# Five places of a streamed hybrid encoder layer: a flush of put-off work, copies of T, steps around the solve, the sums of one post, loads of the embedding blocks

## The chip, the cores and the metric

The kernel runs on one core of a Trainium2 chip. The metric is the device time of one execution in microseconds (us); smaller is better. A core has a matrix engine (TensorE, PE in the profile; its weight loads are PEld), VectorE (DVE), ScalarE (ACT), GpSimd (POOL) and SyncE (SP, which here only issues transfers).

## The reference, cut to what matters

512 rows of `x` and 16 meta rows ahead of them make 528 positions of 1024 features. One layer is computed: a layer norm of the embedding, two mixers side by side (stick-breaking attention over 8 heads of 64, and an RWKV-7 recurrence over 8 heads of 64), their gated sum through `w_out`, a layer norm with the residual, a mixture of 16 experts of which each position takes 2, and a last layer norm.

```python
h = layer_norm(concat([meta, x]), emb_ln_g, emb_ln_b)
p = h @ w_in                       # q, k, v, p_rw, gate_sb, gate_rw
o_sb = stick_breaking_attention(q, k, v)
x = p_rw + (token_shift(p_rw) - p_rw) * mu       # r, k, v, wd, ad, gd
w = exp(-DECAY_SCALE * sigmoid(w0 + tanh(wd) @ w_up)); a = sigmoid(a0 + ad @ a_up); g = sigmoid(gd) @ g_up
# for each t:  S = S*w_t + (S @ -kk_t)(kk_t*a_t)^T + v_t k_t^T ;  y_t = S @ r_t
o_rw = (group_norm(y)*lnx_g + lnx_b + (r*k*r_k).sum()*v) * g
merged = sigmoid(gate_sb) * (o_sb @ p_sb) + sigmoid(gate_rw) * (o_rw @ p_rwkv)
h = layer_norm(ALPHA*h + merged @ w_out, ln1_g, ln1_b)
h = layer_norm(ALPHA*h + MoE(h), ln2_g, ln2_b);  return h[16:]
```

## The kernel before

**Products in three parts.** A product in float32 is made of three matmuls on rounded numbers: both sides are split into a high part (`_hi`, a copy that rounds, on ScalarE, line L109) and a low part (`_lo`, what is left, a subtraction on VectorE or GpSimd, line L237), and high by high, high by low and low by high are added up in one bank of TensorE's result memory.

**The stream.** Every large projection from the embedding (and later the merge's) is a job of 8 steps in one list, `ST`. A step (L329) is three matmuls with a 128x128 block of weights. A job has two halves of four steps. At the first step of half h the load of half h+3 is issued on SP (`w_raw`, L267); at the second step half h+2 is split (`w_hi` on ScalarE, `w_lo` on GpSimd, or partly on VectorE where `ST.dve` says so). `ST.later(n, f)` puts a piece of work off until n more steps are issued. So the order in which the program issues work is written out by hand, and each engine runs its own instructions in that order; nothing is rearranged on the chip.

**drive.** Stages that leave TensorE idle (RWKV's preparation, the solve, the chain, the posts) are generators. `drive` runs such a stage and, at each `yield d`, issues steps until the debt d is paid; a step pays 0.66. A yield of 1.0 thus brings two steps or one, by what is owed already, one of 4.0 six or so. The 16 gate jobs (`gate`, 128 steps) are what is left for the solve and the chain. At the end of a gate job ScalarE makes a sigmoid, GpSimd multiplies it with the attention's part and a transfer writes it to memory.

**The order of the stages.** Attention (18 rounds with six streamed steps each); up to the end of job `xv0`; LoRA's weights and inputs are converted (L703, L704, and L766, L767 in `lora`); RWKV's preparation in four pairs; `solve`; `chain`; the posts; the merge; `w_out`; router; experts. `shift_mix` makes RWKV's shifted inputs: ScalarE scales two banks, and the addition on VectorE (L520) is put off by `MIX` = 2 steps, and frees the banks.

**solve.** It inverts triangular blocks. VectorE makes `T` row by row (L955 to L957). Three copies of it on ScalarE follow (`T0`, twice `Tf`), then VectorE's merges into `Xc` and `Tf`, four transposes (L984, `T32`; L988, the last of `U`), two memsets on GpSimd (L990), which wait for L988 since they write to `U` too, and a yield of `SY[0]`. Then come two rounds of 32 small matmuls each: L1000 (on `LM` and `T32`), a copy on ScalarE, a yield of `SY[1]`, L1010 (on `Xs` and `U`), a copy, a yield of `SY[2]`.

**chain and posts.** `chain` runs the recurrence over nine chunks for two groups of head pairs; it begins with a yield of `CHY[2]`. `post(b)` normalizes 128 positions of the output `ORW`: L1104 to L1112 (mean, square, variance), L1118 (scale and offset), L1119 (add the bonus; on GpSimd for b < 3), L1121 (multiply by the gate; VectorE). Three posts begin within the chain. `posts` ends them, and starts the fourth, and splits `ORW` into `orw_hi` and `orw_lo` (`in_parts`, L1127), parts 0 to 2 on GpSimd, part 3 on VectorE.

**merge.** Jobs `m0` to `m5` work through `MERGES`, pairs of a block m of 128 output columns and a part of the positions (`L1188`; in L1192 to L1195 VectorE multiplies the bank by the gate, adds attention's part, ScalarE makes `hT_hi`, VectorE `hT_lo`). In the loop over m = 0 to 9 ahead of `w_out` (L1311), `wsplit_by` splits the weights of `w_out` in put-off pieces (L1242 on VectorE), `wraw` loads more of them, and at m = 1, 3, 5, 7 (`HBM`) one block of the embedding, `hb[b]`, is loaded back (L1328), and multiplied by `emb_ln_g` and shifted by `emb_ln_b` on VectorE (L1329, L1330), of which the rows are loaded at m = 1. The experts' loads (`fetch`, 1 MB each on SP) begin at m = 7.

Of the kernel before, what the change touches and what calls it, by code (L numbers as in the profile page):

```python
# [13 lines left out]
AF = mybir.ActivationFunctionType  # L14
OP = mybir.AluOpType
# [17 lines left out]
DE = 512  # L33
CAP = 32

CHY = (0.0, 0.66, 4.0, 7)
GS = (2, 3, 4, 7)
PST = 9
YPL = (2, 1)
# [3 lines left out]
MIX = 2  # L43
MD = 4
SOLVE_RATE = 1.0
SY = (1.0, 1.4, 1.4)
WARM = 16
WARM_R = (8, 12)
HSD = 4
OVT = 6  # L50
LY = 6
HBM = (1, 3, 5, 7)
FAT = (7, 7, 8, 9)
WOT = (2, 2), (4, 3), (2, 3)
ROT_W = [0, 1, 3, 6, 7]
# [13 lines left out]
def trunk(ctx, tc, A, out):  # L69
    nc = tc.nc  # L70
# [4 lines left out]
    h_d = dram.tile([SEQ, D], FT, name="h_d")  # L75
# [180 lines left out]
    class Stream:  # L256
# [19 lines left out]
        def step(self):  # L276
            h, u = divmod(self.n, 4)
            if h >= 2 * len(self.jobs):
                return
            if u == 0:  # L280
                self.load(h + 3)
            if u == 1:
                self.split(h + 2)
            self.jobs[h // 2][1](self.w.get(h), self.n % 8)
            self.n += 1
            due = [f for n, f in self.hooks if n <= self.n]
            self.hooks = [k for k in self.hooks if k[0] > self.n]
            for f in due:
                f()

        def run(self, n, upto=None):
# [11 lines left out]
    ST = Stream()  # L303
# [374 lines left out]
    for n in range(18):  # L678
        i = n % 4
# [14 lines left out]
        if 0 <= n - 2 < 16:  # L694
            next(live[n - 2])
    ST.upto("xv0")
    lora_w = AT.tile([128, 2, 512], FT, name="lora_w", bufs=1)
    nc.sync.dma_start(lora_w[0:64, 0], A["w_up"][0])
    nc.sync.dma_start(lora_w[64:128, 0], A["a_up"][0])
# [227 lines left out]
    def solve():  # L927
# [22 lines left out]
        Tf = TB  # L950
        nc.gpsimd.memset(Tf[:, 0:16, 16:32], 0.0)
        pr_ = PX.tile([128, 1024], FT, name="pr", tag="xrk", bufs=2)
        for t in range(2, 16):
# [2 lines left out]
                                    Lc[:, :, t, None, 0:t].to_broadcast([128, 3, t, t]), op=OP.mult)  # L956
            nc.vector.tensor_reduce(T[:, :, t, 0:t], pr, axis=AX.X, op=OP.add)  # L957
            yield 0.4 + t * t * 0.0063
        act(T0[:, :, 16:32], T[:, 2], AF.Copy)
        act(Tf[:, 0:16, 0:16], T[:, 0], AF.Copy)  # L960
        act(Tf[:, 16:32, 16:32], T[:, 1], AF.Copy)
        Xc = RW.tile([128, 16, 16], FT, name="Xc", tag="t_G")

        def merge(dst, x, y, i0, i1, j0, j1, k0, k1):
# [8 lines left out]
        for i in (0, 8):  # L973
            merge(Xc, TA[:, 16:32, 0:16], T[:, 0], i, i + 8, 0, 8, 0, 16)
            yield 2.5
            merge(Xc, TA[:, 16:32, 0:16], T[:, 0], i, i + 8, 8, 16, 8, 16)
            yield 1.45
        for i, n in ((0, 8), (8, 16)):
            for j in range(0, 16, 128 // n):
                merge(Tf[:, 16:32, 0:16], T[:, 1], Xc, i, i + 8, j, j + 128 // n, 0, n)  # L980
                yield 2.5
# [115 lines left out]
    def post(b, room):  # L1097

        ts = slice(128 * b, 128 * b + 128)
        y = ORW[:, :, ts]  # L1100
        four = "p (h t) -> p h t"
        s2, bg = room(b)
        for i in range(2):
            nc.sync.dma_start(bg[i], bg_d[:, i, :, ts].rearrange("h p t -> p h t"))  # L1104
        pm = sm()
        nc.tensor.matmul(pm, bones, y, start=True, stop=True)
        yield YP
        nc.vector.scalar_tensor_tensor(y, pm.rearrange(four, h=4), -1.0 / 64, y, op0=OP.mult, op1=OP.add)
        act(s2, y, AF.Square)
        yield YP  # L1110
        pv = sm()
        nc.tensor.matmul(pv, bones, s2, start=True, stop=True)  # L1112
        act(s2, pv.rearrange(four, h=4), AF.Ln, bias=eps_x, scale=1.0 / 64)
        yield YP
        act(s2, s2, AF.Exp, scale=-0.5)
        nc.vector.tensor_tensor(y, y, s2, op=OP.mult)
        for hp in range(4):
            nc.vector.tensor_scalar(y[:, hp], y[:, hp], col("lnx_g", hp), col("lnx_b", hp), op0=OP.mult, op1=OP.add)  # L1118
        (nc.vector if b == 3 else nc.gpsimd).tensor_tensor(y, y, bg[0], op=OP.add)  # L1119
        yield YP  # L1120
        nc.vector.tensor_tensor(y, y, bg[1], op=OP.mult)  # L1121
        yield YP
# [15 lines left out]
    def posts():  # L1138

        for u in PR[0]["posts"]:  # L1140
            for _ in u:
                pass
        late = post(3, late_room)
        in_parts(0, nc.gpsimd)
        yield YPL[0]
        for i in range(5):
            next(late)
            if i in (0, 2):
                WR.append(wraw(wo_units[i // 2], i // 2))
            if i < 2:  # L1150
                in_parts(i + 1, nc.gpsimd)
            yield YPL[1]
        in_parts(3, nc.vector)

# [161 lines left out]
    for m in range(10):  # L1316
        if m < 8:
            ST.run(m_done[m] - ST.n)
            if m == 0:
                WO.append(wsplit_by(WR.pop(0), *WOT[1]))  # L1320
            if m in (2, 4):
                WR.append(wraw(wo_units[1 + m // 2], 1 + m // 2))
            if m == HBM[0]:
                for nm, t in (("emb_ln_g", egr), ("emb_ln_b", ebr)):
                    nc.sync.dma_start(t, bass.AP(tensor=A[nm].tensor, offset=A[nm].offset, ap=[[0, 128], [1, D]]))
            if m in HBM:
                b = HBM.index(m)
                nc.sync.dma_start(hb[b], h_d[b * 128:(b + 1) * 128, :])  # L1328
                nc.vector.tensor_tensor(hb[b], hb[b], egr, op=OP.mult)  # L1329
                nc.vector.tensor_tensor(hb[b], hb[b], ebr, op=OP.add)  # L1330
            if m == 4:
                WO.append(wsplit_by(WR.pop(0), *WOT[2]))
# [458 lines left out]
    with tc.For_i(0, n_1, 1) as _:  # L1791
# [43 lines left out]
        with tc.For_i(0, n_x, 1) as j:  # L1835
# [52 lines left out]
            y = hb[1]  # L1888
# [45 lines left out]
```

## Time and profile before

| what | value |
|---|---|
| executions shown, us | 889.43, 889.32, 882.3 |
| their median, us | 889.32 |
| the profiled execution, us | 883.24 |
| its span in the profile, us | 881.4 |
| its mean granted TensorE clock | 0.956 |
| busy: TensorE, VectorE, ScalarE, GpSimd | 92%, 48%, 36%, 34% |
| TensorE's weight loads (beside its matmuls) | 60% |

The profile is of one execution. Its span runs from its first instruction to its last. The difference to the execution's time lies around it. Busy shares are over the whole span; the stages differ. PEclk is the TensorE clock that the chip granted, as a share of full speed (1.00 is 2.4 GHz, 0.50 is 1.2 GHz).

### The profile page before, as it was taken

Reading aid. Unit: us, or ns where it says so; the run is one execution under the profiler, and the core shown is the slowest. Engines: PE = TensorE matmul, PEld = TensorE weight load, DVE = VectorE, ACT = ScalarE, POOL = GpSimd, SP = SyncE. Lnnn points to the kernel's source line nnn. Section 1 sums busy time; section 2 is a strip of 40 time slices with the busy share of each in tenths; the row PEclk is TensorE's granted clock in tenths of the full one; section 3 lists DMA queues with packets and bytes.
Section 4 is the critical chain, followed back from the end, with each engine's and each line's share of the span. In section 5 each row is a group of like instructions: output and inputs, shape, how many; then the busy total and the mean of one; then the engine's idle time right before and its main releaser. Section 6 shows DMA issues by size and latency. Waiting matters only on the chain. (4 is left out here: it accounts for less than half of the span.)

```text
span 881.4 us, 16057 instructions
## 1 busy us (share of the span) xinstructions
PE 807.7 (92%) x6476; PEld 527.5 (60%) x6476; DVE 421.5 (48%) x791; ACT 317.7 (36%) x639; POOL 299.5 (34%) x343
## 2 busy tenths in 40 slices
PE   7989899879998989979997889999999999999993
PEld 6877777867888867757665777783333333333331
DVE  7565664741467669982464668730112212302304
ACT  6465565554666575435455222111010010010000
POOL 4265765751442444865454000111101300300102
PEclk8998898999999999989999899989999999999996
DMA  4511111135433225434226679689799999999800
GB/s 148 189 51 49 48 49 49 48 100 203 147 98 97 84 74 156 126 115 132 62 62 199 221 247 368 252 314 331 247 387 387 371 386 387 378 385 387 316 1 27
DMA packets 127234, 169.17 MB, mean 192 GB/s; under 512 B 7106, under 2 KB 62476, under 8 KB 127156
## 3 DMA queue, kind: packets, MB, share of 16 engines
q1 hardware_dynamic: 122228, 158.00, 52.1%
q10 hardware_dynamic: 2944, 5.90, 1.8%
q0 software_dynamic: 1984, 4.21, 1.4%
q8 instruction: 52, 0.85, 0.4%
q14 instruction: 26, 0.21, 0.1%
HBM read 152.29 MB, written 17.89 MB: 193 GB/s over the span
## 5 line engine op out<-in xcount | busy, mean ns | idle before, releaser
L237 POOL TENSOR_TENSOR w_lo<-w_raw,w_hi 128x512 fp32r<-128x512 f32 x87 | 119.8, 1378 | 160.4 <-ACT w_hi L109 147.8
L1710 PE MATMUL bank<-raw,x 128*32 128x512 f32 x1536 | 170.8, 594 | 1.9 <-ACT hid L109 1.2
L329 PE MATMUL bank<-hT_hi,w_hi 128*128 128x264 f32 (+1 forms) x512 | 149.4, 348 | 4.1 <-ACT w_hi L109 2.7
L329 PE MATMUL bank<-hT_hi,w_lo 128*128 128x264 f32 (+1 forms) x512 | 139.1, 328 | 4.4 <-POOL w_lo L237 4.4
L329 PE MATMUL bank<-hT_lo,w_hi 128*128 128x264 f32 (+1 forms) x512 | 138.1, 326 | 0.0
L1710 PEld LDWEIGHTS bank<-raw,x 128*32 128x32 f32 x1536 | 47.6, 110 | 105.1 <-issue 102.6
L329 PEld LDWEIGHTS bank<-hT_hi,w_hi 128*128 128x128 f32 x512 | 87.6, 194 | 18.9 <-ACT w_hi L109 4.2
L329 PEld LDWEIGHTS bank<-hT_hi,w_lo 128*128 128x128 f32 x512 | 87.5, 194 | 11.6 <-POOL w_lo L237 6.5
L329 PEld LDWEIGHTS bank<-hT_lo,w_hi 128*128 128x128 f32 x512 | 87.3, 194 | 7.5
L1721 PE MATMUL bank<-raw,h 128*32 128x512 f32 x768 | 87.0, 594 | 0.0
L1684 POOL TENSOR_TENSOR ln_f<-ln_f,mhalf 128x1 f32<-128x1 f32 x12 | 11.5, 955 | 184.6 <-DVE ln_f L1683 184.6
L109 ACT ACTIVATE w_hi<-w_raw 128x512 fp32r<-128x512 f32 x100 | 62.3, 624 | 18.7 <-DMA w_raw<-in_w_in_dram 6.5
L1639 DVE SCALAR_TENSOR_TENSOR hid<-hid,gat,bank 128x512 f32<-128x512 f32 x12 | 9.0, 747 | 121.2 <-PE bank L1710 64.5
L1721 PEld LDWEIGHTS bank<-raw,h 128*32 128x32 f32 x768 | 23.4, 110 | 50.8 <-issue 50.8
L562 POOL TENSOR_TENSOR R<-zs,R 128x144 f32<-128x144 f32 (+3 forms) x32 | 44.9, 1421 | 19.1 <-DVE R L560 19.1
L1311 PE MATMUL bank<-raw,hT_hi 128*128 128x512 f32 x128 | 45.5, 412 | 2.7 <-ACT hT_hi L109 2.7
L109 ACT ACTIVATE h<-bank 128x512 f32<-128x512 f32 x12 | 7.2, 597 | 97.5 <-PE bank L1629 97.5
L109 ACT ACTIVATE x<-bank 128x512 f32<-128x512 f32 x14 | 8.4, 597 | 82.8 <-PE bank L1629 74.3
L1457 POOL TENSOR_TENSOR ln_rs<-ln_ve,mhalf 128x1 f32<-128x1 f32 x4 | 5.3, 1328 | 89.9 <-DVE ln_ve L1456 89.9
L109 ACT ACTIVATE hid<-bank 128x512 f32<-128x512 f32 x12 | 7.1, 595 | 72.2 <-PE bank L1710 72.2
L560 DVE TENSOR_TENSOR_SCAN R<-ones_r,ab 128x144 f32<-128x144 f32 (+3 forms) x32 | 31.8, 1035 | 0.0
L1613 POOL DMA_INDIRECT hb<-h_d,idx x12 | 12.4, 1029 | 54.1 <-DVE idx L1591 36.9
(349 smaller groups left out, 1352.7 us busy)
## 6 DMA issues: line engine op xcount, KB each, us to landing
raw<-in_exp_w_gate_dram SPq DMA_DIRECT2D x32, 1024.0 KB
raw<-in_exp_w_up_dram SPq DMA_DIRECT2D x32, 1024.0 KB
raw<-in_exp_w_down_dram SPq DMA_DIRECT2D x32, 1024.0 KB
w_raw<-in_w_in_dram SPq DMA_DIRECT2D x84, 256.0 KB
raw<-in_w_out_dram SPq DMA_DIRECT2D x4, 1024.0 KB
sig_d<-sg ACTq DMA_DIRECT2D x8, 264.0 KB
sig<-sig_d SPq DMA_DIRECT2D x8, 264.0 KB
xin<-in_x_dram SPq DMA_DIRECT2D x4, 512.0 KB
```

Source lines behind the costliest of these rows:

```text
L109: ins = nc.scalar.activation(out, in_, func, **kw)
L237: eng.tensor_tensor(lo[:, ks], raw[:, ks], hi[:, ks].bitcast(FT), op=OP.subtract)
L329: nc.tensor.matmul(pt[:, :e - s], w_[:, k % 4, :], m[:, k, s:e], start=(k == 0 and n == 0), stop=(k == KD - 1 and n == 2))
L560: nc.vector.tensor_tensor_scan(R[:, h, :W][:, ::-1], ones_r[:, :W], ab[:, h, :W][:, ::-1], 0.0, op0=OP.mult, op1=OP.add)
L562: nc.gpsimd.tensor_tensor(R[:, h, :W], z[:, h], R[:, h, :W], op=OP.subtract)
L1311: nc.tensor.matmul(pt, MG[x][:, k, 128 * b:128 * b + 128], w[y][:, k % 4, :], start=(k == 0 and i == 0), stop=(k == 7 and i == 2))
L1457: nc.gpsimd.tensor_tensor(rs, ve, mhalf, op=OP.pow)
L1613: nc.gpsimd.indirect_dma_start(out=t[:idx.shape[0]], out_offset=None, in_=src, in_offset=bass.IndirectOffsetOnAxis(ap=idx.bitcast(U32), ax ...
L1639: nc.vector.scalar_tensor_tensor(hid, hid, gate, pu, op0=OP.mult, op1=OP.mult)
L1684: nc.gpsimd.tensor_tensor(rs, ve, mhalf, op=OP.pow)
L1710: nc.tensor.matmul(P[k[0]][32 * i:32 * i + 32], x_of(t, i, kk), W[k, e][0][:, s], start=kk == 0, stop=kk == 7)
L1721: nc.tensor.matmul(Y[g, p // 2][r:r + 32], H[t][:, s, 32 * i:32 * i + 32], W[unit_of(k, i), e][0][:, s], start=s == 0 and not second, stop ...
```

## The change

Five edits. First, `ST.flush()`, a new method that runs all work put off so far, is called right behind `ST.upto("xv0")`. Second, the three copies of `T` on ScalarE move behind the merges into `Xc` (four yields later). Third, `SY[0]` goes from 1.0 to 5.0 and `CHY[2]` from 4.0 to 0. Fourth, the sum L1119 of post 2 goes from GpSimd to VectorE, and the low parts 0, 1 and 2 too; the parts 0 and 1 are issued ahead of the call that makes post 3, part 2 at its turn i = 1. Fifth, the loads of the embedding blocks and of the two rows get their own places, m = 0, 1, 3, 5 (`HBL`) and the rows m = 0, while the products stand at m = 2, 3, 5, 7 (`HBM`).

```diff
--- before.py
+++ after.py
@@ -33,7 +33,7 @@
 DE = 512
 CAP = 32
 
-CHY = (0.0, 0.66, 4.0, 7)
+CHY = (0.0, 0.66, 0.0, 7)
 GS = (2, 3, 4, 7)
 PST = 9
 YPL = (2, 1)
@@ -43,13 +43,13 @@
 MIX = 2
 MD = 4
 SOLVE_RATE = 1.0
-SY = (1.0, 1.4, 1.4)
+SY = (5.0, 1.4, 1.4)
 WARM = 16
 WARM_R = (8, 12)
 HSD = 4
 OVT = 6
 LY = 6
-HBM = (1, 3, 5, 7)
+HBL, HBM = (0, 1, 3, 5), (2, 3, 5, 7)
 FAT = (7, 7, 8, 9)
 WOT = (2, 2), (4, 3), (2, 3)
 ROT_W = [0, 1, 3, 6, 7]
@@ -286,6 +286,12 @@
             due = [f for n, f in self.hooks if n <= self.n]
             self.hooks = [k for k in self.hooks if k[0] > self.n]
             for f in due:
+                f()
+
+        def flush(self):
+
+            due, self.hooks = self.hooks, []
+            for _, f in due:
                 f()
 
         def run(self, n, upto=None):
@@ -694,6 +700,7 @@
         if 0 <= n - 2 < 16:
             next(live[n - 2])
     ST.upto("xv0")
+    ST.flush()
     lora_w = AT.tile([128, 2, 512], FT, name="lora_w", bufs=1)
     nc.sync.dma_start(lora_w[0:64, 0], A["w_up"][0])
     nc.sync.dma_start(lora_w[64:128, 0], A["a_up"][0])
@@ -956,9 +963,6 @@
                                     Lc[:, :, t, None, 0:t].to_broadcast([128, 3, t, t]), op=OP.mult)
             nc.vector.tensor_reduce(T[:, :, t, 0:t], pr, axis=AX.X, op=OP.add)
             yield 0.4 + t * t * 0.0063
-        act(T0[:, :, 16:32], T[:, 2], AF.Copy)
-        act(Tf[:, 0:16, 0:16], T[:, 0], AF.Copy)
-        act(Tf[:, 16:32, 16:32], T[:, 1], AF.Copy)
         Xc = RW.tile([128, 16, 16], FT, name="Xc", tag="t_G")
 
         def merge(dst, x, y, i0, i1, j0, j1, k0, k1):
@@ -975,6 +979,9 @@
             yield 2.5
             merge(Xc, TA[:, 16:32, 0:16], T[:, 0], i, i + 8, 8, 16, 8, 16)
             yield 1.45
+        act(T0[:, :, 16:32], T[:, 2], AF.Copy)
+        act(Tf[:, 0:16, 0:16], T[:, 0], AF.Copy)
+        act(Tf[:, 16:32, 16:32], T[:, 1], AF.Copy)
         for i, n in ((0, 8), (8, 16)):
             for j in range(0, 16, 128 // n):
                 merge(Tf[:, 16:32, 0:16], T[:, 1], Xc, i, i + 8, j, j + 128 // n, 0, n)
@@ -1116,7 +1123,7 @@
         nc.vector.tensor_tensor(y, y, s2, op=OP.mult)
         for hp in range(4):
             nc.vector.tensor_scalar(y[:, hp], y[:, hp], col("lnx_g", hp), col("lnx_b", hp), op0=OP.mult, op1=OP.add)
-        (nc.vector if b == 3 else nc.gpsimd).tensor_tensor(y, y, bg[0], op=OP.add)
+        (nc.vector if b > 1 else nc.gpsimd).tensor_tensor(y, y, bg[0], op=OP.add)
         yield YP
         nc.vector.tensor_tensor(y, y, bg[1], op=OP.mult)
         yield YP
@@ -1140,15 +1147,16 @@
         for u in PR[0]["posts"]:
             for _ in u:
                 pass
+        in_parts(0, nc.vector)
+        in_parts(1, nc.vector)
         late = post(3, late_room)
-        in_parts(0, nc.gpsimd)
         yield YPL[0]
         for i in range(5):
             next(late)
             if i in (0, 2):
                 WR.append(wraw(wo_units[i // 2], i // 2))
-            if i < 2:
-                in_parts(i + 1, nc.gpsimd)
+            if i == 1:
+                in_parts(2, nc.vector)
             yield YPL[1]
         in_parts(3, nc.vector)
 
@@ -1320,12 +1328,14 @@
                 WO.append(wsplit_by(WR.pop(0), *WOT[1]))
             if m in (2, 4):
                 WR.append(wraw(wo_units[1 + m // 2], 1 + m // 2))
-            if m == HBM[0]:
+            if m == 0:
                 for nm, t in (("emb_ln_g", egr), ("emb_ln_b", ebr)):
                     nc.sync.dma_start(t, bass.AP(tensor=A[nm].tensor, offset=A[nm].offset, ap=[[0, 128], [1, D]]))
+            if m in HBL:
+                b = HBL.index(m)
+                nc.sync.dma_start(hb[b], h_d[b * 128:(b + 1) * 128, :])
             if m in HBM:
                 b = HBM.index(m)
-                nc.sync.dma_start(hb[b], h_d[b * 128:(b + 1) * 128, :])
                 nc.vector.tensor_tensor(hb[b], hb[b], egr, op=OP.mult)
                 nc.vector.tensor_tensor(hb[b], hb[b], ebr, op=OP.add)
             if m == 4:
```

## Rows read from the trace of the kernel before

**Rows 1.** Busy us, share of the span and instructions of each engine.
```profile
PE 807.7 (92%) x6476; PEld 527.5 (60%) x6476; DVE 421.5 (48%) x791; ACT 317.7 (36%) x639; POOL 299.5 (34%) x343
```

**Rows 2.** Waits of PE: who waits <- for what: us, times, longest.
```profile
PE bank L1000 <- DVE T L984: 5.7, 1, 5.7
...
PE bank L329 <- POOL w_lo L237: 4.4, 5, 1.0
...
PE bank L1188 <- DVE w_lo L237: 3.4, 2, 3.0
...
PE bank L1188 <- POOL orw_lo L1127: 3.1, 1, 3.1
...
PE bank L1311 <- ACT hT_hi L109: 2.7, 1, 2.7
...
PE bank L329 <- ACT w_hi L109: 2.7, 5, 1.0
```

**Rows 3.** Windows: stretch, us, PE busy (instructions), granted clock, DMA share, GB/s.
```profile
386.90:393.60 6.70, 5.79 (x110) 0.50 0.13 39
...
393.70:475.50 81.80, 76.37 (x979) 1.00 0.34 104
...
399.60:406.60 7.00, 7.00 (x30) 1.00 0.24 75
...
502.90:506.20 3.30, 3.30 (x9) 0.50 0.10 30
...
571.20:581.30 10.10, 9.33 (x42) 0.50 0.48 163
```

**Rows 4.** Timeline, 192 to 198 us: start, us busy, instruction [idle before <- releaser].
```profile
192.77 1.84 DVE L767 TENSOR_TENSOR lx<-lora_x,lx 128x528 fp32r<-128x528 f32 x1
...
196.68 0.89 DVE L520 SCALAR_TENSOR_TENSOR xv<-bank,cols,xv 128x264 f32<-128x264 f32 x2
...
197.31 0.47 PE L658 MATMUL bank<-osb_hi,w_hi 128*128 128x512 f32 x1 [2.92 <-DVE xv L520]
```

**Rows 5.** Timeline of the solve, four engines.
```profile
362.23 0.42 ACT L109 ACTIVATE T<-T 128x256 f32<-128x256 f32 x1 [5.42 <-DVE T L957]
...
385.65 2.01 DVE L984 STREAM_TRANSPOSE T<-TB 128x1024 f32<-128x1024 f32 x1
...
391.33 1.93 POOL L990 MEMSET U<- 32x1024 f32 x2 [5.93 <-DVE U L988]
...
393.33 1.27 POOL L237 TENSOR_TENSOR w_lo<-w_raw,w_hi 128x512 fp32r<-128x512 f32 x1
...
398.39 1.20 PE L1010 MATMUL bank<-U,Xs 32*32 32x32 f32 x64
```

**Rows 6.** Timeline of the posts.
```profile
468.67 1.11 DVE L1118 TENSOR_SCALAR orw<-orw,cols 128x128 f32<-128x128 f32 x4
...
471.18 1.76 DVE L1121 TENSOR_TENSOR orw<-orw,y_bg 128x512 f32<-128x512 f32 x1 [1.39 <-POOL orw L1119]
...
476.39 1.91 PE L1112 MATMUL bank<-y_s,bones_r 128*128 128x512 f32 x2
...
483.72 0.69 DVE L1127 TENSOR_TENSOR orw_lo<-orw,orw_hi 128x512 fp32r<-128x512 f32 x1 [0.69 <-ACT orw_hi L109]
```

**Rows 7.** Waits of L1329 on transfers (us, times), and the merge's timeline.
```profile
  DMA hb<-h_d: 8.9, 3
...
483.42 0.97 SPq L267 DMA_DIRECT2D w_raw<-in_p_rwkv_dram  x2
...
490.77 0.43 SPq L1328 DMA_DIRECT2D hb<-h_d  x1
...
493.37 1.47 DVE L1242 TENSOR_TENSOR raw<-raw 128x512 fp32r<-128x512 f32 x2
...
499.12 1.23 DVE L1329 TENSOR_TENSOR hb<-hb,raw 128x1024 f32<-128x1024 f32 x1 [4.28 <-DMA hb<-h_d]
```

**Rows 8.** Windows of the expert stage (columns as in rows 3).
```profile
837.00:866.00 29.00, 28.76 (x266) 1.00 0.00 1
```

## The prediction, made before the kernel after was run

> **What bounds the kernel now.** I read the page's busy shares first. TensorE works 807.7 of 881.4 us, the next engine less than half [rows 1], so what matters is why TensorE stops and how fast it is clocked. Its list of waits, sorted by length, comes second: the longest single waits are one for a transposed T in the solve, one for a weight's low part and one for hT_hi in the merge, one for the low part of the attention output's partner `orw_lo`, and about 1 us each for `w_hi` and `w_lo` [rows 2]; one of 2.92 for `xv` stands in the timeline [rows 4]. These are the waits that the diff touches. Third, the granted clock by stretches. After several of these waits the chip runs TensorE at 1.2 GHz (PEclk 0.50) for a while: a stretch of 6.7 us behind the solve's wait, and four of about 3.3 us, of which one row stands, behind the two waits of `posts` and the two of the merge [rows 3]. A stretch at half clock does half the work, so 3.3 us of it cost 1.65. Last, the expert stage: from 837 to 866 us the transfers are over and TensorE is busy for 28.8 of 29 us [rows 8]. The expert weights thus land some 29 us ahead of the end, and a gain won before that stage reaches the end unless it exceeds that.
>
> **The flush.** Before, the put-off mixing of `xv` (L520) stands on VectorE behind all conversions of the LoRA weights and inputs, and starts at 196.68; TensorE waits 2.92 for the bank that it frees [rows 4]. After, L520 (0.89) goes ahead of them, and the bank is free long before TensorE asks at 197.3 - 2.9 = 194.4. Late next is what was pushed back: the low part of `lx` (L767), ready at 192.77 + 1.84 = 194.61 [rows 4], now at least 0.89 later, 195.5. TensorE has two streamed steps first. A step is three matmuls, 30 take 7.00 us [rows 3], so 0.70 each: it asks at 194.4 + 1.4 = 195.8. L520 must itself wait for ScalarE's scaling, so I count 0.3 lost. Gain **2.6**, bounds 1.5 (L767 took 1.84 for a tile twice the width of L520's 0.89 for two; held like that again, about 1.1 more is lost) and 2.9. The clock is full here; nothing comes from it.
>
> **T's copies and the solve's steps.** These go together, because both only fill time before one fixed event. VectorE works on T until L984 ends at 385.65 + 2.01 = 387.66, and TensorE, with its steps done, waits 5.7 for it [rows 2, 5]. ScalarE stands 5.42 at the copies [rows 5], which costs TensorE the two waits of 1.0 for `w_hi` and `w_lo` [rows 2]. Issued 12 steps later, the copies find T ready: but TensorE then only comes earlier to L1000 and waits longer. Alone: 0. The steps: SY[0] from 1.0 to 5.0 issues 4.0/0.66 = 6 more steps ahead of L1000 (each with three matmuls; with each four of them a split on ScalarE and GpSimd and a load on SP, with each eight a product on GpSimd and two transfers). CHY[2] from 4.0 to 0 takes 7 away behind the solve. Undisturbed, the chain would start 7 x 0.70 = 4.9 earlier.
>
> It is disturbed. The memsets L990 stand on GpSimd ahead of the yield, and wait for VectorE's last transpose of U: 391.33 to 393.26 [rows 5]. The split of half 22 (step 81 of the gates) was issued behind L990 before too, and finished at 393.33 + 1.27 = 394.60 [rows 5], in good time, for TensorE needed it only in the 7 steps ahead of the chain. After the change steps 81 to 86 stand ahead of L1000, step 87 behind it, and step 88, the first of half 22, ahead of L1010. TensorE gets there some 4 us after 387.66 and must wait until 394.60, about 3 us. From there: rest of the step 0.5, L1010 1.20, two steps 1.4, L1000 (as many matmuls as L1010) 1.2, two steps 1.4, L1010 1.2, three steps 2.1; together 9.0, so the chain starts at 403.6, where it started at 399.6 + 7.0 = 406.6 [rows 3, 5]. 3.0 won. Two waits in a row keep the clock low: the half-clock stretch that ended at 393.6 [rows 3] may outlast 394.6 by some 2 us, which costs 1.1. GpSimd's work ahead of L990 is the same as before, so VectorE's chain to 387.66 is put at no change. Gain **1.9**; bounds -1 (a whole further stretch of 6.7 us at half clock, 3.35, and 0.6 of slip on VectorE) and 4.9. The seventh step, now run later, is put at 0: it falls into `posts`' wait for the last part of `orw_hi`, which stays; without that cover it costs 0.70.
>
> **Post 2 and the second parts.** Before, GpSimd does post 2's sum and the low parts 0, 1 and 2, with a weight split between, and TensorE stands 3.1 for them [rows 2]. After, VectorE does them. It is free at 468.67 + 1.11 = 469.78 [rows 6]; L1119, L1121 and two L1127 are four instructions of 0.69 (VectorE's own L1127 [rows 6]) with 0.02 between, 2.84, and one block by GpSimd's split of 0.7: 473.3. Behind these on VectorE waits L1108 of post 3, for which ScalarE's square and TensorE's L1112 wait: 0.7 and 0.7, so L1112 starts at 474.7 and, at full clock, takes half of its 1.91 [rows 6]: 475.7, against 476.39 + 1.91 = 478.3. Everything up to the last low part hangs on L1112, so this moves as a whole: **2.5** (2.6 less 0.1 for the later first `orw_lo`). Bounds 1.0 (blocked twice) and 5.0 (not blocked, and no half-clock stretch behind the wait that stays, 1.65).
>
> What a block costs here is in the trace: L1121 took 1.76 beside GpSimd's L1127 and 0.69 is what its like takes alone [rows 6]. The Trainium skill, SBUF — State Buffer, section "SBUF: two separate sides", says that VectorE instructions with two SBUF inputs and GpSimd instructions hold a shared port pair exclusively, the loser standing still for the whole instruction. By that rule each split left on GpSimd in this stretch could block a moved instruction, two of them: the part would be 1.0 and the sum 14.0 instead of 15.5; the trace agrees with the rule by the 1.07 more of L1121.
>
> **The block loads.** Before, each product L1329 on VectorE waits for a load issued just before it: 8.9 us in three waits [rows 7]. Queued behind the first are a weight's low part and the multiplication by the gate, and for these TensorE waits 3.4 (two times) and 2.7 [rows 2], and runs two stretches of 3.3 at half clock [rows 3]: 3.4 + 2.7 + 3.3 = 9.4 on TensorE. After, the loads go out one to two blocks ahead of their product. The first took 499.12 - 490.77 = 8.35 to land [rows 7]; issued at m = 0, right behind the loads of 483.42 [rows 7], say 484.4 to 485.9, it lands by 494, while VectorE comes to its product only after block 2, some six instructions of 0.69 and one wait of 0.69 behind 493.37 + 1.47 = 494.8 [rows 6, 7]: about 499. On SP three issues are moved ahead of the loads for block 2 and of a `p_rwkv` load; they need SP some 1.3 us. Late next is VectorE itself: without the 8.9 it is at work all the time from the last post to `half_in`, and it cannot give more than 8.9 back. I take **8.5**, bounds 3.0 and 9.4.
>
> Sum: 2.6 + 1.9 + 2.5 + 8.5 = **15.5**. The profiled execution took 883.24 (its span 881.4 and 1.84 around it), which makes 867.7. The runs shown have their median 6.1 above the profiled one; all four executions have their mean at 886.1, 2.8 above. I put the forecast that much above the sum: **870.5**.
>
> **Rivals.** *The loads collide.* The embedding rows and block 0, 1.5 MB issued early, hold up the loads for blocks 2 and 3, and VectorE waits at L1192 instead of L1329. For: 8.35 us of landing now, which shows a queue. Against: VectorE needs block 2's loads only 6 us after their issue. Price 5: 872.7 in the profile's terms. The Trainium skill, DMA: Bandwidth & Descriptors, section "Issuing engines are not separate DMA queues", has all transfers run on the same 16 engines and interleave, which is how an early load would slow a needed one; no row of before shows the pair.
> *No hold in the solve.* If half 22's split gets through, the whole 4.9 comes: 864.7. Against it is the order on GpSimd [rows 5].
> *Mostly moved, not removed.* The solve gives nothing and the loads collide: 2.6 + 0 + 2.5 + 3.5 = 8.6: 874.6, within 1%.
> *Slower.* The low clock outlasts the solve. In the chain no streamed work stands ahead of the first groups any more, and between 393.7 and 475.5 TensorE's 76.4 us of work ran at 1.00 [rows 3]. Each us at half clock loses half a us, so from 31 us on the gain is gone; through the whole stretch it would be 867.7 + 76 = 944. Against: the longest such stretch beside work is 10.1 us [rows 3].
>
> **How the numbers follow.** About 1% (8.9 us) is what a measurement of this kernel tells from no change. Forecast (11 to 20 won) 0.62, colliding loads 0.14 (of it 0.03 within 1%), no hold 0.09, mostly moved 0.10, slower 0.05. Faster 0.82, same 0.13, slower 0.05. The range runs from no hold at the lower runs, 864.7 less 3, to mostly moved with runs 5 to 6 above the profile: 861.5 to 880.
>
> **What would show it.** No wait of L658 on L520; ScalarE's 5.42 gone; TensorE in one wait before L1000 and a new one of about 3 us in L329 on L237 right behind L990; `orw_lo`'s wait below 1.5; no wait of L1329 on a transfer, and VectorE without gaps from 484 to 545. The forecast is wrong if waits on transfers turn up at L1192, if PEclk stays at 0.50 in the chain, or if TensorE begins to wait for expert weights.

## The result and the profile after

| | before | changed |
|---|---|---|
| median of four executions each, us | 888.58 | 876.54 |
| range, us | 882.3 to 889.43 | 873.92 to 877.38 |
| ratio of the times | | 0.9865, 95% interval 0.9826 to 0.9904 |
| the profiled execution, us (span) | 883.24 (881.4) | 873.92 (872.2) |

The change makes the kernel 12.0 us faster in the medians (1.35%) and 9.3 us in the profiled executions. The forecast was 870.5 in a range of 861.5 to 880. The executions of one kernel differ mostly by how long the granted clock stood at 1.2 GHz: the kernel before ran from 880.7 to 894.9 us in four groups of runs, with mean clocks of 0.943 to 0.964 (one slow execution of 898.3 left out), and its profiled execution of 883.24 is among its quicker ones. Over all executions that were taken, 38 before and 8 of the changed kernel, the medians are 889.2 and 875.8, which is 13.4 apart.

The page of the changed kernel, first part (busy us, share of the span, instructions):

```profile
PE 804.0 (92%) x6476; PEld 522.4 (60%) x6476; DVE 422.0 (48%) x795; ACT 317.2 (36%) x639; POOL 294.2 (34%) x339
```

Against [rows 1] nothing is saved in work: four instructions went from GpSimd to VectorE, and TensorE's busy time fell by 3.7 us only. TensorE's waits in the changed kernel (who waits <- for what: us, times, longest):

```profile
PE bank L335 <- POOL w_lo L237: 8.0, 8, 2.9
...
PE bank L1007 <- DVE T L991: 3.5, 1, 3.5
...
PE bank L1196 <- DVE orw_lo L1134: 1.9, 2, 1.6
...
PE bank L1475 <- DVE hb L1457: 1.8, 2, 1.5
...
PE bank L1319 <- ACT hT_hi L109: 0.4, 1, 0.4
```

Of the waits of [rows 2], the one of the merge's `w_lo` fell from 3.4 to 0.3 and that for `hT_hi` from 2.7 to 0.4; `orw_lo` went from 3.1 to 1.9, and the one for T from 5.7 to 3.5. The one for `xv` of [rows 4] is gone. New are 2.9 of L335 for `w_lo`, and 1.5 of L1475 for the residual sum `hb`.

Where the 9.2 us of span went is read from windows, cut at the same instructions of both kernels: first product of the attention's output, first of RWKV's preparation, its last, first of the chain, last mean of the posts (L1106, now L1113), first and last product of `w_out`, end. Before (stretch, us, TensorE busy (instructions), granted clock, DMA share, GB/s):

```profile
188.74:228.97 40.23, 36.19 (x174) 1.00 0.59 198
228.97:338.25 109.28, 101.05 (x776) 1.00 0.29 88
338.25:406.68 68.43, 60.59 (x475) 0.93 0.43 131
406.68:471.46 64.78, 62.43 (x778) 1.00 0.30 88
471.46:490.24 18.78, 13.86 (x77) 0.82 0.60 199
490.24:568.41 78.17, 71.78 (x343) 0.96 0.84 298
568.41:881.40 312.99, 294.12 (x2738) 0.96 0.83 303
```

The changed kernel, the same stretches:

```profile
186.83:224.26 37.43, 36.21 (x174) 1.00 0.63 213
224.26:335.09 110.83, 102.66 (x776) 0.98 0.29 87
335.09:403.83 68.74, 60.59 (x469) 0.90 0.44 135
403.83:469.32 65.49, 62.62 (x778) 1.00 0.25 72
469.32:487.24 17.92, 14.58 (x82) 0.81 0.79 257
487.24:558.39 71.15, 68.68 (x343) 1.00 0.92 325
558.39:872.20 313.81, 294.06 (x2738) 0.96 0.83 302
```

Column by column: the flush's stage gives 2.8; the preparation loses 1.5 to one stretch at half clock (0.98 in the clock's column); solve up to the chain gives nothing (-0.3), the chain loses 0.7, the posts give 0.9, the merge with `w_out` gives 7.0, the rest loses 0.8. The stretch ahead of the first row gives 1.9; the change does not touch it.

The chain has the same 778 products in both kernels, so its 0.7 is not a further step. It is a new wait of TensorE for ScalarE's work on a gate (`g_st`). TensorE's waits, before and after:

```profile
PE bank L329 <- ACT g_st L109: 0.3, 1, 0.3
```
```profile
PE bank L335 <- ACT g_st L109: 1.0, 2, 0.7
```

The seventh step stands in the posts: of the stream's products (L329, now L335) three fall between the last mean and `w_out` before, six after (windows of that line alone, before and after):

```profile
471.46:490.24 18.78, 0.69 (x3) 0.82 0.60 199
```
```profile
469.32:487.24 17.92, 1.40 (x6) 0.81 0.79 257
```

The solve, TensorE's timeline (start, us, instruction, idle before <- releaser):

```profile
384.83 1.92 PE L1007 MATMUL bank<-T,LM 32*32 32x32 f32 x64 [3.52 <-DVE T L991]
...
388.12 0.63 PE L335 MATMUL bank<-hT_hi,w_hi 128*128 128x512 f32 x1
391.68 0.80 PE L335 MATMUL bank<-hT_hi,w_lo 128*128 128x512 f32 x1 [2.93 <-POOL w_lo L237]
```

and GpSimd's:

```profile
388.35 1.93 POOL L997 MEMSET U<- 32x1024 f32 x2 [9.21 <-DVE U L995]
390.36 1.26 POOL L237 TENSOR_TENSOR w_lo<-w_raw,w_hi 128x512 fp32r<-128x512 f32 x1
```

GpSimd stands idle for 9.2 us in front of the memsets with the needed split right behind them: the wait that the prediction named, with its size. What follows in TensorE's clock (windows, columns as above):

```profile
384.80:398.00 13.20, 10.24 (x158) 0.50 0.26 79
398.10:470.00 71.90, 69.03 (x910) 1.00 0.26 76
473.00:480.00 7.00, 6.33 (x24) 0.51 0.84 298
```

The half clock behind T's wait lasts 13.2 us against 6.7 [rows 3], 6.4 of them behind the second wait. In the posts one stretch of 7.0 stands where the kernel before had two of about 3.3, the same in sum. The merge, which had two stretches behind its waits, has none (1.00 in its row above).

### The profile page after: what moved, and what is told of

The parts are those of the page before. It is cut to its first block, busy times and chain, and to the rows that moved or that the text cites. A ratio compares the mean times of both kernels' runs of the same rounds, so it can differ in the third digit from the quotient of the medians.

```text
span 872.2 us, 16061 instructions
## 1 busy us (share of the span) xinstructions
PE 804.0 (92%) x6476; PEld 522.4 (60%) x6476; DVE 422.0 (48%) x795; ACT 317.2 (36%) x639; POOL 294.2 (34%) x339
## 5 line engine op out<-in xcount | busy, mean ns | idle before, releaser
L237 POOL TENSOR_TENSOR w_lo<-w_raw,w_hi 128x512 fp32r<-128x512 f32 x87 | 123.4, 1421 | 169.1 <-ACT w_hi L109 151.2
L335 PE MATMUL bank<-hT_hi,w_hi 128*128 128x264 f32 (+1 forms) x512 | 149.1, 347 | 3.4 <-ACT w_hi L109 1.6
L335 PE MATMUL bank<-hT_hi,w_lo 128*128 128x264 f32 (+1 forms) x512 | 138.6, 327 | 8.0 <-POOL w_lo L237 8.0
L335 PE MATMUL bank<-hT_lo,w_hi 128*128 128x264 f32 (+1 forms) x512 | 137.2, 324 | 0.0
L335 PEld LDWEIGHTS bank<-hT_hi,w_hi 128*128 128x128 f32 x512 | 87.1, 193 | 18.3 <-ACT w_hi L109 2.7
L335 PEld LDWEIGHTS bank<-hT_hi,w_lo 128*128 128x128 f32 x512 | 86.8, 193 | 16.5 <-POOL w_lo L237 11.6
L335 PEld LDWEIGHTS bank<-hT_lo,w_hi 128*128 128x128 f32 x512 | 86.5, 192 | 7.2
L556 DVE COPY zs<-bank 128x264 f32<-128x264 f32 (+3 forms) x40 | 15.3, 432 | 33.9 <-ACT ab L109 33.8
```

The source lines that it names most:

```text
L237: eng.tensor_tensor(lo[:, ks], raw[:, ks], hi[:, ks].bitcast(FT), op=OP.subtract)
L335: nc.tensor.matmul(pt[:, :e - s], w_[:, k % 4, :], m[:, k, s:e], start=(k == 0 and n == 0), stop=(k == KD - 1 and n == 2))
L556: nc.vector.tensor_copy(zs[:, h, s:e], pz[h][:, :e - s])
```

## The experiments

All are edits of the changed kernel. Times are medians of all executions; the kernel before had medians of 889.32 (16 executions), 889.66 (7) and 888.39 (11) beside the three groups. The changed kernel with its repetition has eight executions, 872.9 to 877.4, with the median 875.8.

| label | what differs from the changed kernel | us (executions) | ratio to before, 95% interval |
|---|---|---|---|
| no_flush | no flush | 883.11 (7) | 0.9938 (0.9907 to 0.9968) |
| no_solve | copies of T, SY, CHY as before | 873.78 (4) | 0.9807 (0.9764 to 0.9851) |
| memset_late | memsets behind the yield | 873.05 (4) | 0.9816 (0.9774 to 0.9857) |
| no_loads | block loads as before | 883.53 (10) | 0.9947 (0.9917 to 0.9976) |
| after_again | nothing | 874.31 (4) | 0.9832 (0.9765 to 0.9899) |
| no_post | post 2 and low parts as before | 875.71 (4) | 0.9856 (0.9787 to 0.9926) |
| copies_only | SY and CHY as before | 874.08 (4) | 0.9835 (0.9754 to 0.9916) |
| hb3_late | memset_late, block 3's product later | 870.17 (4) | 0.9789 (0.9723 to 0.9855) |
| hb3_late_more | the same | 870.16 (6) | 0.9775 (0.9729 to 0.9822) |
| hb3_only | block 3's product later | 871.89 (6) | 0.9802 (0.9765 to 0.9838) |
| hb3_no_solve | the same, and no_solve | 870.59 (6) | 0.9799 (0.9763 to 0.9835) |
| hb3_no_flush | hb3_late without the flush | 876.43 (6) | 0.9860 (0.9815 to 0.9905) |

**The flush.**

```diff
     ST.upto("xv0")
-    ST.flush()
```

> The changed kernel without the flush, all else kept. If the trace's reading holds (the first matmul of the LoRA products, L779, moved from 1.9 us early to 5.1 us early, so the flush is worth about 2.8), the wait of L664 on xv of 2.9 us returns and the time is 2.8 above the changed kernel's 876.5: 879.3. If the gain came from chance in the attention's clock instead, the time is 876.5 to 877.5, whether the wait returns or not.

> hb3_late without the flush. All seven traces with the flush took 37.4 us from the first product of the attention's output to RWKV's preparation, the two without 40.2 and 39.7: by that 2.3 to 2.8 slower, 872.5 to 873. But the changed kernel without the flush was 6.6 to 8.8 slower than with it in the medians, with 4 to 5 us more lost to the clock over the span, for which this stage shows no cause. If the flush does bear on the clock of later stages, the time is 876.8 to 879.

Taken away, the stage takes 39.7 and 40.0 us, with it 37.4 in every trace but one (37.0 in no_loads; windows, columns as above, of no_flush and then of hb3_no_flush):

```profile
188.70:228.40 39.70, 36.17 (x174) 1.00 0.59 200
```
```profile
187.50:227.50 40.00, 36.13 (x173) 1.00 0.59 199
```

So 2.3 to 2.8 is the flush's own in this stage. The times move by more: 7.3 (883.11 less 875.8) and 6.3 (876.43 less 870.16). Span times mean clock, an estimate of the time at full clock, differs by 2.2 and 3.5 on average; the rest is time at half clock over the whole span. The single traces show no cause: stretches at half clock in the preparation come with the flush (no_loads, two of 7 us from 241 to 280) and without it (no_flush, one of 7 us from 243 to 250), and the traces differ as much in the attention, ahead of the flush. Both profiled executions without the flush (879.54 and 869.21) were also the quickest of their kernel, so the traces show little of what the medians lose. What the flush does to the clock behind it is not settled.

**The loads.**

```diff
-HBL, HBM = (0, 1, 3, 5), (2, 3, 5, 7)
+HBL, HBM = (1, 3, 5, 7), (1, 3, 5, 7)
...
-            if m == 0:
+            if m == 1:
                 for nm, t in (("emb_ln_g", egr), ("emb_ln_b", ebr)):
```

> The changed kernel with the loads of the embedding blocks and rows issued where they were before (at m = 1, 3, 5, 7), all else kept. The traces' reading: from the first matmul of w_out to its last 7.0 us were won, so 876.5 + 7.0 = 883.5, with waits of the product on hb of about 9 us in three and a wait of L1196 on w_lo near 3. The forecast's 8.5 would give 885.0. If the stretches at half clock moved by chance in the merge, 881.5 to 882.5 (the two waits of 2.7 and 2.3 alone).

Measured 883.53, 7.7 above the changed kernel. The old waits are back (TensorE's waits of no_loads):

```profile
PE bank L1196 <- DVE w_lo L237: 2.8, 1, 2.8
PE bank L1319 <- ACT hT_hi L109: 2.4, 1, 2.4
```

and the product L1339 waits for its transfer, as in [rows 7]:

```profile
  DMA hb<-h_d: 6.8, 3
```

With the loads early, L1339 waits for no transfer at all: the first follows the merge's work (L1203, at 497.24) without a gap (VectorE's timeline of the changed kernel):

```profile
497.84 1.22 DVE L1339 TENSOR_TENSOR hb<-hb,raw 128x1024 f32<-128x1024 f32 x1
```

**Copies and steps.** copies_only undoes the steps alone, by this edit; no_solve also puts the three copies of `T` back ahead of the merges.

```diff
-CHY = (0.0, 0.66, 0.0, 7)
+CHY = (0.0, 0.66, 4.0, 7)
-SY = (5.0, 1.4, 1.4)
+SY = (1.0, 1.4, 1.4)
```

> The changed kernel with the copies of T, SY[0] and CHY[2] as before, all else kept. The forecast had these three at 1.9 us won: undoing them would give 878.4. The reading of the two traces: from the end of RWKV's preparation (3.16 us early) to the chain's start (2.85 early) nothing was won, and ScalarE's exponential of post 2 comes about 1 us later behind a weight's copy that the moved steps put there. By that the kernel is 875.5 to 876.5, the same or up to 1 us faster. A rival: the clock decides; before, one stretch at half clock of 6.7 us follows the wait, after, one of 13.2; if the longer stretch is chance, undoing costs 1.9 or more and the time is over 878.

> The changed kernel with SY[0] and CHY[2] as before; the copies of T stay late. Without all three, the kernel took 873.8. The forecast's step 'the copies alone: 0' gives 873.8 again, with a longer wait of L1007 for T than the 5.2 of that kernel (the copies' 5.4 and 1.0 now fall into it), and then the moved steps alone cost 2.7. If instead the copies are what costs, the time is 876.5.

873.78 and 874.08, beside 875.8 with the moved steps: they win nothing, and may cost 1 to 2. The copies alone are worth 0, as forecast: the medians of the two kernels without the steps lie 0.3 apart, less than their executions scatter. Where the copies' waits went is seen in copies_only:

```profile
PE bank L1007 <- DVE T L991: 11.1, 1, 11.1
```

From 5.2 in no_solve this wait grew to 11.1: TensorE only comes earlier to the same event. The stage from the end of the preparation to the chain took 68.4, 71.9, 69.6 and 69.3 us in the four traces without the moved steps, and 68.7 to 72.4 in the six with them and with the memsets where the change has them.

**The hold on GpSimd.**

```diff
-        for r in (32, 96):
-            nc.gpsimd.memset(U[r:r + 32, :, 0:32], 0.0)
         nc.vector.transpose(T0, T0)
         yield SY[0]
+        for r in (32, 96):
+            nc.gpsimd.memset(U[r:r + 32, :, 0:32], 0.0)
```

> The changed kernel with the two memsets of U (L997) issued behind the yield of SY[0], so that the split of half 22 stands ahead of them on GpSimd. Theory: the hold on GpSimd costs the 2.9 us that L335 waits for w_lo, and this second wait keeps TensorE at half clock from 391.6 to 398 us, 3.2 more. Then the 2.9 wait goes, the stretch at half clock ends about 6.6 us after the wait for T, as before, and the kernel takes 876.5 - 2.9 - 1.6 to 3.2 = 870.4 to 872. Rival: TensorE has other work behind the wait which now waits instead (L1017 for U), or the clock stays low in any case; then 874 to 876.5.

873.05, 2.8 less than the changed kernel: between the theory's 870.4 to 872 and the rival's 874 to 876.5. The 2.9 us wait is gone and the wait for T has grown: it is 3.5 in two of the six traces with the hold, 6.3 in the other four, and 7.3 here (TensorE's waits of memset_late):

```profile
PE bank L1007 <- DVE T L991: 7.3, 1, 7.3
...
PE bank L335 <- POOL w_lo L237: 4.4, 6, 0.8
```

From the preparation's end to the chain it takes 66.2 us, where the changed kernel took 68.7 and its repetition 72.2 (windows of memset_late, then of after_again):

```profile
335.51:401.73 66.22, 57.91 (x471) 0.92 0.46 140
```
```profile
334.23:406.47 72.24, 62.07 (x470) 0.86 0.43 128
```

Over all traces this stage took 68.7 to 72.4 us with the hold (six) and 63.7 to 68.3 without it (four): the hold's cost is clear there, though the intervals of the medians overlap.

**The repetition.**

> The changed kernel itself once more, beside the others of this call. 876.5 and within 1 of it by every theory; it tells how far the medians of separate calls can be compared, and whether the stretch at half clock of 13 us behind the wait for T (384.8 to 398 us) is there again (two of two theories: it is, since a second wait follows the first).

874.31, with half clock from 383 to 403 us. The stretch behind the two waits was 14 to 20 us long in all six traces that have the hold. But a second wait is not needed for a long one: in the four traces without the hold it lasted 10, 14, 14 and 3 us, and in no_solve and copies_only, where no long wait follows the one for T (5.2 and 11.1), 14 too. The 6.7 of the kernel before was a short one. Windows of the repetition and of hb3_late, which has no second wait:

```profile
383.00:403.40 20.40, 15.09 (x232) 0.50 0.26 78
```
```profile
384.00:398.00 14.00, 11.03 (x204) 0.51 0.17 49
```

**Post 2 and the low parts.**

```diff
-        (nc.vector if b > 1 else nc.gpsimd).tensor_tensor(y, y, bg[0], op=OP.add)
+        (nc.vector if b == 3 else nc.gpsimd).tensor_tensor(y, y, bg[0], op=OP.add)
...
-        in_parts(0, nc.vector)
-        in_parts(1, nc.vector)
         late = post(3, late_room)
+        in_parts(0, nc.gpsimd)
...
-            if i == 1:
-                in_parts(2, nc.vector)
+            if i < 2:
+                in_parts(i + 1, nc.gpsimd)
```

> The changed kernel with post 2's sum and the low parts 0 to 2 back on GpSimd, all else kept. The forecast had these at 2.5 us: 879.0. The traces' reading: the last product with the variance (L1119) ends only 0.4 closer to the chain than before, since a stretch at half clock stands there as before; by that 876.9 to 877.9. A rival: the gain is in the clock behind it too, 1.65 for a stretch of 3.3 us that goes or comes: up to 880.6.

875.71, within 0.1 of the changed kernel's 875.8: next to the moved steps this part brings nothing that can be measured. The traces of the other kernels tell why. From the last mean of the posts to `w_out`, the kernel before took 18.8 us; no_post, with the moved steps and without this part, 18.9; with both, 17.4 to 19.4 in nine traces (18.8 on average); with this part and without the moved steps (no_solve, copies_only, hb3_no_solve), 15.7, 15.6 and 15.6. So the part is worth 3.1 against the one trace that has neither, 1.7 of it by one stretch of 3.4 us at half clock less, and the moved steps take it back. By the traces, what they do is on ScalarE; no run moved that work by itself. In copies_only (ScalarE's timeline):

```profile
464.50 0.69 ACT L109 ACTIVATE y_s<-bank,eps_x 128x512 f32<-128x512 f32 x1 [0.53 <-PE bank L1119]
465.22 0.63 ACT L109 ACTIVATE y_s<-y_s 128x512 f32<-128x512 f32 x1
```

and in the changed kernel:

```profile
464.44 0.69 ACT L109 ACTIVATE y_s<-bank,eps_x 128x512 f32<-128x512 f32 x1 [1.26 <-PE bank L1119]
465.03 0.62 ACT L109 ACTIVATE w_hi<-w_raw 128x512 fp32r<-128x512 f32 x1
465.55 0.62 ACT L109 ACTIVATE g_st<-g_st 128x512 f32<-128x512 f32 x1
466.07 0.62 ACT L109 ACTIVATE y_s<-y_s 128x512 f32<-128x512 f32 x1
```

A weight's copy and a gate's exponential, which come with a step, stand between the logarithm and the exponential of post 2, so the exponential starts 1.6 instead of 0.7 behind its logarithm, and all of post 2 with it. The same two instructions delay the exponential of post 3, which starts 1.62 instead of 0.70 behind its logarithm, and one more streamed step (0.7) stands between the last mean and the merge. Of the 2.35 us between these two traces, 1.1 lie ahead of the variance of post 3, 0.4 in that product (at half clock here) and 0.8 behind it. The changed kernel's exponential of post 3, on ScalarE:

```profile
475.78 0.69 ACT L109 ACTIVATE y_s<-bank,eps_x 128x512 f32<-128x512 f32 x1 [0.50 <-PE bank L1119]
...
477.40 0.62 ACT L109 ACTIVATE y_s<-y_s 128x512 f32<-128x512 f32 x1
```

The longer half clock of this trace (7.0 against 3.5 us) is not the reason: the repetition had 3.4 in the posts and took 18.8.

**The residual sum.** On the kernel with the late memsets:

```diff
-HBL, HBM = (0, 1, 3, 5), (2, 3, 5, 7)
+HBL, HBM = (0, 1, 3, 5), (2, 3, 5)
...
-    for n in range(4, 11):
+    for n in range(4, 8):
         fetch()
-    for b in range(4):
+    for b in range(3):
         half_in(b, 0, PZ[b])
...
             if k == 4 and b:
                 logits(b - 1, 1)
+            if k == 5 and b == 1:
+                nc.vector.tensor_tensor(hb[3], hb[3], egr, op=OP.mult)
+                nc.vector.tensor_tensor(hb[3], hb[3], ebr, op=OP.add)
+                half_in(3, 0, PZ[3])
+                for n in range(8, 11):
+                    fetch()
```

> The kernel with the late memsets (873.1), and the product of the fourth embedding block and its first residual sum moved behind those of the other blocks, into VectorE's idle 2.9 us at 539 to 542 (three expert loads, which use the same buffer, move behind it). Theory: the loads' gain fell 1.5 short of the forecast because VectorE, busy without a gap from the merge on, gives the second residual sum of block 0 late, for which L1475 waits 1.5 us. Then this wait goes and the time is 871.5; with the 3.7 us that the clock loses there, in that kernel, from 533 to 540 gone too, 868. Rival: the wait only moves to a later residual sum: 873.

870.17, 2.9 below memset_late, and 870.16 when repeated. In the changed kernel the wait looks so (TensorE's timeline):

```profile
534.82 0.65 PE L1475 MATMUL bank<-ident,hb 128*128 128x128 f32 x4 [1.54 <-DVE hb L1457]
```

In hb3_late it is not there, and `w_out` takes 67.8 us from its first to its last product, 73.7 in memset_late. Of the 5.9, 3.4 were lost in a stretch of 6.8 us at half clock (533 to 540 us), which memset_late, no_solve and copies_only had and none of the five traces with the edit; the two traces of the changed kernel hadn't it either, so only 2.5 can be put down to the edit. The edit on the changed kernel alone (hb3_only, below) is worth 3.9 in the medians (875.8 less 871.89), more than the 1.5 us of the wait: the stretch behind `w_out` is shorter too, 310.9 to 313.2 us in the five traces with the edit (three of them near 311) against 313.0 to 313.8 in the others.

**What each is worth in the end.** hb3_late once more, and without the late memsets, and without the moved steps too:

> The same kernel as hb3_late, in more rounds and beside the three others of this call, which each take one thing from it: 870.2, within 1.

> The changed kernel with the fourth embedding block's product late, and the memsets of U where the change has them (ahead of the yield). The hold on GpSimd costs, by the traces of five kernels with it and two without, 70.0 - 67.2 = 2.8 us from the end of RWKV's preparation to the chain's start. So 870.2 + 2.8 = 873.0. Rival: freeing GpSimd only lets it stand in VectorE's way (T comes 1.0 us later in both kernels without the hold); then 870 to 871.

> As hb3_only, but with the copies of T, SY[0] and CHY[2] as before the change. From the end of the preparation to the chain's start three kernels without the moved steps took 70.0 on average, and five with them and with the hold 70.0 too; the mean with the chain to the last product of the fourth post is 0.7 better without them (64.8 against 65.5, in every trace). So 0 to 1 us faster than hb3_only: 872 to 873. The forecast's 1.9 would have it 1.9 slower: 874.9.

870.16, 871.89 and 870.59. The late memsets are worth 1.7 here, less than the 2.8 expected; the intervals overlap. Without the moved steps, the kernel is 1.3 faster than with them and with the hold, about as expected, and as quick as with them and without the hold: with the hold gone the steps win about 3 us up to the chain (63.7 to 68.3 against 68.4 to 71.9), and lose 0.7 in the chain and some 3 in the posts. What the hold's end costs is seen in GpSimd's work while VectorE makes T. hb3_only (GpSimd busy in the stretch, from VectorE's first transpose to T32):

```profile
334.18:387.40 53.22, 36.04 (x24) 0.98 0.48 144
```

hb3_late:

```profile
332.63:386.82 54.19, 43.21 (x27) 0.98 0.54 160
```

Three more instructions of GpSimd fall into it, and T comes 1.0 later. hb3_late beats both kernels: 18 us (2.2%, interval 1.8 to 2.7) below the one before and 5.6 below the changed one.

## Why the prediction was right, and where not

The direction was right, the range holds the time, and the sum was too large: 15.5 forecast, 9.3 in the profiled executions, 12.0 in the medians of four and 13.4 in those of all executions. By its own steps:

- **The flush, 2.6: right in its stage**, which gives 2.8. The loss of 0.3 behind it came: a weight load of the first LoRA product (L779) waits 0.32 for `lx`. "The clock is full here; nothing comes from it" holds for the stage, but in the medians the flush is worth 6 to 7, and the cause of the rest is open.
- **The copies, 0: right**, shown by copies_only. **The steps, 1.9: wrong.** The new wait was named with its place and its cause, and its size was right (2.93 for "about 3"). What was mis-sized is the clock behind it. The prediction let the half clock outlast the wait by 2 us, 1.1 lost; it lasted 6.4, a loss of 3.2. 3.0 less 3.2 is -0.2, and the stage gave -0.3. Why the half clock lasts so long is not shown; that it takes two waits in a row is not borne out, since it lasted 10 to 14 us around one wait in six other traces.
- **The seventh step, 0: wrong.** Its cover, the posts' wait for `orw_hi`, was said to stay. The step stands in the posts with its 0.7, and the work on ScalarE that the moved steps bring delays the exponentials of posts 2 and 3 by 0.9 each. The chain is longer too, 65.5 against 64.8 us in every trace, by TensorE's wait for `g_st`, which is 1.0 in all ten traces with the moved steps and 0.3 in all four without. The prediction counted TensorE's matmuls of the step, not what the steps put in front of ScalarE's chain.
- **Post 2 and the low parts, 2.5: right alone, wrong in this company.** 3.1 without the moved steps; with them 0.9 in the two profiled executions and 0.1 on average over nine traces. One instruction was blocked by GpSimd's split, though none of the four that were counted: the four L1125 took 2.09 instead of the 1.11 of [rows 6], at the same time as a split. `orw_lo`'s wait fell to 1.6, not below 1.5. The Trainium skill, SBUF — State Buffer, section "SBUF: two separate sides", has a port pair held for a whole instruction; the trace agrees with its 0.98 lost. The case of two blocks, which would have made the part 1.0, did not come; the 0.9 has the moved steps for its cause.
- **The loads, 8.5: right in the mechanism, 1.5 too large.** L1339 waits for nothing, `w_lo` and `hT_hi` come in time, both stretches at half clock are gone: 7.0. Missing is the new wait of 1.5 for VectorE's residual sum. The prediction said that VectorE would work without a gap up to `half_in`, and did not go on to ask who waits for `half_in`. The gaps are not all gone, either: VectorE stands 0.7 for ScalarE's `hT_hi` at each of the eight `hT_lo`, and is without a gap only from 523 to 537 us, where the sums are.

So 2.8 - 0.3 - 0.7 + 0.9 + 7.0 = 9.7, and with what the change does not touch (1.9 won ahead of it, 1.5 lost in the preparation, 0.8 behind `w_out`) 9.3. The two stretches of clock outside of the change, 1.9 and 1.5, are chance as far as these traces show. In the medians the parts taken away one by one give 7.3 (flush), 7.7 (loads), -0.1 (post 2 and low parts) and -2.1 (copies and steps), 12.8 together. So that the time came within 6 us of the forecast is in part luck: the flush's unexplained 4 us or so stand in for what the solve and the posts did not give, and without them it would have lain near 880, the end of the range.

**The rivals.** That the loads collide was not seen: no L1339 and no L1200 waited for a transfer. That there is no hold in the solve is refuted by the 9.21 of the memsets. That the clock stays low through the chain is refuted too: 398 to 470 us ran at 1.00. "Mostly moved, not removed" came true in its first half: the solve gave nothing, but the loads did not collide.

**The forecast's last step.** To get from the profiled execution to the median, 2.8 was added, from four executions. With 34 more of the kernel before, its medians are 5.2 to 6.4 above the profiled one. With that the forecast would have been 873 to 874, against a median of 875.8 over eight executions.

## What to carry to other kernels

When a wait is filled with work brought forward, list what that work issues on every engine at its new place, and what then comes later at its old one: here the steps cost TensorE 0.7 and yet, by the traces, took away the gain of another edit through ScalarE's queue. Price a new wait together with the clock behind it, and take that price from several traces: one trace of before showed 6.7 us at half clock, others of nearly the same code 10 to 14. And when an engine becomes busy without a gap, its next consumer behind the stage is the next wait.

## What the runs showed of the hardware

How long TensorE stays at 1.2 GHz around a wait scatters widely: around one long wait for T, of 4.4 to 11.1 us, it was 3 to 14 us in eight traces; where a wait of 2.9 followed a few us later, 14 to 20 in six. That the second wait adds to it fits, but the two ranges touch, and 14 us came with and without it. Nor does the stretch end as soon as TensorE works again: in hb3_late it worked without a gap from T's arrival at 387.0 on, steps and rounds of 32x32 products in turn, and stayed at 1.2 GHz for 10.8 us more (window):

```profile
386.97:397.80 10.83, 10.83 (x194) 0.50 0.02 5
```

What ended it is not shown. The same kernel's executions lie up to 14 us apart (881 to 895), and their mean granted clock goes with it (0.964 at 881.6 us, 0.952 at 892.5), so that one profile of each of two kernels could be wrong by half of the effect sought here.

VectorE and GpSimd hinder each other in the solve by whole instructions. A split (L237) that takes 1.27 us by itself took 3.03 beside VectorE's products over T, of which one, begun beside GpSimd's instruction before it (L645, 374.85 to 376.15), took 2.98 where its like took 1.99; the split ends 1.2 us behind that product (timelines of GpSimd and VectorE in the changed kernel):

```profile
376.11 3.03 POOL L237 TENSOR_TENSOR w_lo<-w_raw,w_hi 128x512 fp32r<-128x512 f32 x1
```
```profile
375.01 2.98 DVE L972 TENSOR_TENSOR pr<-T,Xc 128x1024 f32<-128x1024 f32 x1
...
379.29 1.99 DVE L972 TENSOR_TENSOR pr<-T,Xc 128x1024 f32<-128x1024 f32 x1
```

T's stretch on VectorE took 51.6 to 54.2 us for the same 48 instructions, the longest three with 27 instead of 24 of GpSimd's in it (a fourth with 27 took 52.7).
